# Twelve of sixteen experts in 64-slot pairs of plain float32 products, in turn with four split ones

## The chip, the cores and the metric

The program runs on one core of a Trainium2 chip. The metric is the device time of one execution in microseconds; the median of several executions is taken. Five engines run their own instruction streams beside each other: TensorE (PE, with its weight loads shown as PEld), VectorE (DVE), ScalarE (ACT), GpSimd (POOL) and SyncE (SP), which here issues the loads of the weights.

## What is computed

Two transformer blocks follow one another on 256 tokens of width 1024. The first has three token mixers and, behind them, a mixture of experts in two levels; the second has two layers with modulation from a conditioning vector. The change touches only the mixture of experts of the first block. Each token goes to one of four groups and, in it, to two of four experts:

```python
def hier_moe(h, wg, bg, we, be, w_gate, w_up, w_down):
    t = h.reshape(-1, D)                                  # 256 x 1024
    g_onehot = one_hot(argmax(t @ wg + bg), N_GROUPS)     # 4 groups, top 1
    ...                                                   # top 2 of the group's 4 experts
    y = jnp.zeros_like(t)
    for e in range(N_EXPERTS):                            # 16
        hid = jax.nn.silu(t @ w_gate[e]) * (t @ w_up[e])  # 1024 -> 256
        y = y + gates[:, e:e + 1] * (hid @ w_down[e])     # 256 -> 1024
    return y
```

All of it is float32. The inputs are drawn from a fixed seed; counted from them, the groups take 52, 33, 132 and 39 tokens, and their experts 25, 22, 40, 17; 18, 14, 19, 15; 32, 59, 82, 91; and 25, 11, 22, 20.

## The kernel before, in words

**Precision.** The kernel makes the product of two float32 matrices from three products in the type `float32r`: both operands are split into a high and a low part, and high x high, high x low and low x high are summed in PSUM. For a weight, ScalarE copies the high part (`hi`, L313) and VectorE subtracts it for the low part (`lo`, L317), in `split` (L300), from the raw tile that a DMA has brought (`raw`, 1 MB). Three pools hold the raw, high and low tiles; `rings` sets their number, (4, 4) in this stage: four raws and four each of hi and lo. `piece` takes a raw from a list of already loaded ones, or allocates one and issues its DMA on SyncE's queue, which waits there until the buffer is free.

**Routing.** `Moe.route` finds each token's group and experts, the group with most tokens and the order of the groups, which SyncE loads into registers, since the addresses of the weights hang on it. As soon as the first group is known, it issues four weight loads (L1659). Each token gets a slot, and `Pm` is the 0/1 matrix from tokens to slots. The largest group has four tiles of 128 slots, one for each expert. Each of the other three groups has one tile of 128 slots, which its four experts share: every one of them computes all slots, and its gate is zero where a token is not its own.

**Overflow.** If an expert of the largest group has, or another group has, over 128 tokens, `further` handles the rest under an `If` (L1813): a body of four experts written out one after the other.

**Gather, experts, scatter.** `gathered` multiplies the tokens (in high and low parts, `hh` and `hw`) by `Pm` and gives 8 chunks of 128 features for 512 slots (32 products of 512 columns), and later, at the fifth expert, for 384 slots (32 products of 384 columns). `slot_gates` multiplies `Pm` by the gates, 14 products (L1834). Then 16 experts run one after the other, and TensorE's order is laid by the scheduler along this list: `expert_in`, 8 chunks x 3 products of 512 columns (gate and up side by side, L1731 to L1733); `expert_out`, with the activation, two transposes (L1744), and 2 chunks x 2 halves x 3 products (L1754 to L1756), one expert behind. `rows_out` splits the result, and `scatter` (L1790) multiplies it by the transposed `Pm` and adds it to the residual `XT` (L1796): once for the four tiles of the largest group after its last expert, and once for the other three at the end. Behind it the first feed-forward part of the second block begins (`early`, product at L604), whose weights are issued at L297 as raws of a new pool.

The modulation products (`ada_mm`, L1060) are the one place of the kernel that already uses plain float32 products on a part of the columns of TensorE: 32 output rows each, up to four side by side.

Of the kernel before, what the change touches and what calls it, by code (L numbers as in the profile page):

```python
# [23 lines left out]
NC = 8  # L24
# [67 lines left out]
def _constants():  # L92
# [42 lines left out]
    k["iota"] = np.tile(np.arange(384, dtype=f) - 4095, (P, 1))  # L135
# [89 lines left out]
class Net:  # L225
# [406 lines left out]
    def first_block(self):  # L632
# [25 lines left out]
        self.ada_pool()  # L658
        es2, moe.T = self.phase("moe1")
# [899 lines left out]
class Moe:  # L1559
# [4 lines left out]

    def __init__(self, net, T):
        self.net, self.T, self.T0 = net, T, T
        nc = net.nc
        self.grep = T([P, 2 * D], "m8", 6)[:, :D]
        nc.sync.dma_start(self.grep, net.ap["grep"])
        self.hh, self.hw = T([P, 2, D], "m8", 6, F32R), T([P, 2, D], "m8", 6, F32R)  # L1570
        self.iota = T([P, 384], "iota")
        nc.sync.dma_start(self.iota, net.ap["k_iota"])
# [6 lines left out]
        self.pt = None  # L1579

# [22 lines left out]
    def route(self):  # L1603
# [4 lines left out]
        G = lambda a: a[:, :, :, None].to_broadcast([P, 2, 4, 5])  # L1608
# [13 lines left out]
        def first_max(src, m=None):  # L1622
# [9 lines left out]
            return m, oh  # L1632


        gm, goh = first_max(gl)
        cho = s(4, 5, dt=BF)
        V.tensor_copy(cho[:, :, :, 4], goh)
# [3 lines left out]
        for t in range(2):  # L1641
            nc.tensor.matmul(pk[:, 60:64], ones, cho[:, t, :, 4], start=(t == 0), stop=(t == 1))
# [11 lines left out]
        V.tensor_copy(order, qf)  # L1654
        load = lambda i: nc.values_load(order[0:1, i:i + 1], engines=(mybir.EngineType.SP,), min_val=0, max_val=3)
# [9 lines left out]
        em, o1 = first_max(se)  # L1665
# [7 lines left out]
        _, o2 = first_max(e2)  # L1673
        V.tensor_tensor(o1, o1, o2, OP.add)
        V.tensor_tensor(cho[:, :, :, 0:4], goh[:, :, :, None].to_broadcast([P, 2, 4, 4]),
                        o1[:, :, None, :].to_broadcast([P, 2, 4, 4]), OP.mult)
# [3 lines left out]
        nc.tensor.matmul(pk[:, 0:20], tri[:, 0:P], c0, start=True, stop=True)  # L1680
        nc.tensor.matmul(pk[:, 20:40], tri[:, P:256], c0, start=True, stop=False)
        nc.tensor.matmul(pk[:, 20:40], tri[:, 0:P], c1, start=False, stop=True)
        nc.tensor.matmul(pk[:, 40:60], ones, c0, start=True, stop=False)
        nc.tensor.matmul(pk[:, 40:60], ones, c1, start=False, stop=True)
# [9 lines left out]
        cnt = pk[:, 40:60].rearrange("p (g e) -> p g e", g=4)  # L1694
        V.tensor_reduce(sm, cnt[:, :, 0:4], AX.XY, OP.max)
        self.more = T([P, 1], "more", 1, I32)
        V.tensor_scalar(self.more, sm, 128.5, None, OP.is_gt)

        big, u, w = T([P, 4], "big"), T([P, 4], "cu"), T([P, 4], "cw_")
        V.tensor_scalar(big, gi[:, 0:4], b, None, OP.is_equal)  # L1700
        V.scalar_tensor_tensor(u, gi[:, 0:4], b, gi[:, 0:4], OP.is_gt, OP.subtract)
        V.tensor_scalar(w, big, -32.0, 32.0, OP.mult, OP.add)
        V.tensor_tensor(u, u, w, OP.add)
        pl5, place = s(4, 5), s(5)
        V.tensor_tensor(pl5, pk[:, 0:40].rearrange("p (t g e) -> p t g e", t=2, g=4), cho, OP.mult)
        V.tensor_reduce(place, pl5.rearrange("p t g e -> p t e g"), AX.X, OP.add)
        inb, ru, tmp = s(1), s(1), s(4)
        V.tensor_tensor(tmp, goh, big[:, None, :].to_broadcast([P, 2, 4]), OP.mult)
        V.tensor_reduce(inb, tmp, AX.X, OP.add)
        tmp2 = s(4)  # L1710
        V.tensor_tensor(tmp2, goh, u[:, None, :].to_broadcast([P, 2, 4]), OP.mult)
        V.tensor_reduce(ru, tmp2, AX.X, OP.add)
        self.slot = s(5)
        ob = s(4)
        V.tensor_tensor(ob, o1, B(inb), OP.mult)
        V.scalar_tensor_tensor(self.slot[:, :, 0:4], ob, -4096.0, place[:, :, 0:4], OP.mult, OP.subtract)
        V.scalar_tensor_tensor(self.slot[:, :, 4:5], ru, -128.0, place[:, :, 4:5], OP.mult, OP.subtract)

    def gate_up(self, w, e, j):
        return self.net.ap["egu"][bass.ds(w * 8 + (2 * e + j), 1)].rearrange("a p n -> (a p) n")  # L1720

    def expert_in(self, w, e, xh, xl, raw=None):
# [3 lines left out]
        for j in range(2):  # L1726
            for hi, lo, ks in net.piece(self.gate_up(w, e, j), 4, 512, raw):
# [8 lines left out]
    def expert_out(self, w, e, pg, gs, y, first, last, raw=None):  # L1736
# [3 lines left out]
        net.act(s, pg[:, 0:256], AF.Silu, scale=gs[:, 4:5])  # L1740
# [200 lines left out]
```

## Time and profile before

| what | value |
|---|---|
| median of 3 runs | 1452.15 us (1451.53 to 1452.27) |
| the profiled execution's own time | 1456.9 us |
| its span | 1455.1 us, mean granted clock 0.988 |
| TensorE, VectorE, ScalarE busy | 1411.1, 1138.2, 856.0 us |
| expert stage, first gate/up product to last scatter | 193.08 to 361.40 us |

The profile is of one execution, 4.75 us longer than the median. The span is the time between its first and last instruction. Busy time is the time in which an engine executes; instructions of TensorE overlap in its pipeline, so the time from one start to the next tells what one costs in a row, and the mean duration is longer.

### The profile page before, as it was taken

To read this page: it belongs to the slowest core of one execution; us is meant where nothing else is said; L and a number is where in the kernel's file an instruction comes from. 1 tells how busy PE (TensorE), PEld (TensorE's weight loads), DVE (VectorE), ACT (ScalarE), POOL (GpSimd) and SP (SyncE) were. 2 spreads that over 40 slices of the span, in tenths; PEclk is the share of its full clock that TensorE was granted. 3 is DMA by queue.
4 is the path that set the end of the run, shared out by engine and by line. 5 is a ranking of instruction groups with operands and counts; after the bars stand their busy time and mean duration, and the time that the engine had idled before them with its cause. 6 is when DMAs were issued, how large, how long until landed. Compare 5 with 4: busy or idle time off the path is not lost.

```text
span 1455.1 us, 22278 instructions
## 1 busy us (share of the span) xinstructions
PE 1411.1 (97%) x8093; PEld 1145.8 (79%) x8093; DVE 1138.2 (78%) x2557; ACT 856.0 (59%) x1575; POOL 0.2 (0%) x4
## 2 busy tenths in 40 slices
PE   7999699999999999999999999999999999999997
PEld 6755478778888888676788889888888677888886
DVE  8996478888999667485899886998687586887664
ACT  7545277777756555364755555666555464766553
POOL 0000000000000000000000000000000000000000
PEclk9999889999999999999999999999999999999999
DMA  8734557887887557543388686787477552275452
GB/s 306 276 129 165 236 202 261 298 324 275 326 318 271 198 184 266 194 169 116 136 294 309 226 297 214 284 315 261 159 263 290 211 194 87 90 241 191 158 179 69
DMA packets 51396, 326.67 MB, mean 224 GB/s; under 512 B 6209, under 2 KB 7378, under 8 KB 18898
## 3 DMA queue, kind: packets, MB, share of 16 engines
q1 hardware_dynamic: 50994, 325.00, 61.6%
q8 instruction: 65, 1.06, 0.3%
q14 instruction: 49, 0.40, 0.1%
q10 hardware_dynamic: 288, 0.20, 0.1%
HBM read 324.13 MB, written 1.05 MB: 223 GB/s over the span
## 4 chain that ended last, share of the span: by engine, by line
PE 79%; DVE 2%; ACT 2%; DMA 1%; issue 0%; DVEq 0%; ACTq 0%; SPq 0%
PE psd L337 12%; PE psa L337 11%; PE pse L337 10%; PE psd L339 7%; PE psa L339 6%; PE pse L339 5%; PE psd L353 2%; PE psm L1060 2%; PE psd L354 2%; PE psd L355 2%; PE psd L1732 1%; PE psd L1733 1%; PE psd L1731 1%; PE pse L1475 1%; PE pse L1754 1%; DVE lo L317 1%
## 5 line engine op out<-in xcount | busy, mean ns | idle before, releaser
L317 DVE TENSOR_TENSOR lo<-raw,hi 128x512 fp32r<-128x512 f32 x992 | 605.1, 639 | 164.9 <-ACT hi L313 162.6
L313 ACT ACTIVATE hi<-raw 128x1024 fp32r<-128x1024 f32 (+3 forms) x498 | 485.1, 980 | 347.7 <-PE psd L337 80.7
L337 PE MATMUL psd<-hl,hi 128*128 128x512 f32 x624 | 225.0, 402 | 7.8 <-ACT hi L313 7.0
L339 PE MATMUL psd<-hl,lo 128*128 128x256 f32 x656 | 185.0, 284 | 0.0
L337 PE MATMUL psa<-hl,hi 128*128 128x512 f32 x464 | 165.2, 397 | 1.2 <-ACT hi L313 1.2
L337 PE MATMUL pse<-hl,hi 128*128 128x512 f32 x464 | 164.3, 396 | 0.0
L337 PEld LDWEIGHTS psd<-hl,hi 128*128 128x128 f32 x624 | 117.9, 190 | 40.1 <-ACT hi L313 8.5
L339 PE MATMUL pse<-hl,lo 128*128 128x256 f32 x512 | 143.0, 280 | 0.0
L339 PE MATMUL psa<-hl,lo 128*128 128x256 f32 x496 | 138.7, 281 | 0.0
L339 PEld LDWEIGHTS psd<-hl,lo 128*128 128x128 f32 x656 | 124.7, 190 | 1.9 <-DVE lo L317 0.9
L337 PEld LDWEIGHTS psa<-hl,hi 128*128 128x128 f32 x464 | 87.2, 188 | 22.6 <-ACT hi L313 1.9
L337 PEld LDWEIGHTS pse<-hl,hi 128*128 128x128 f32 x464 | 87.3, 188 | 20.8 <-ACT w L384 0.3
L339 PEld LDWEIGHTS pse<-hl,lo 128*128 128x128 f32 x512 | 96.5, 189 | 0.2
L339 PEld LDWEIGHTS psa<-hl,lo 128*128 128x128 f32 x496 | 93.6, 189 | 0.8 <-DVE lo L317 0.4
L1089 DVE SCALAR_TENSOR_TENSOR acc<-araw,cact,acc 128x512 f32<-128x512 f32 x118 | 85.8, 748 | 1.6 <-DMA araw<-wada 1.6
L353 PE MATMUL psd<-hi,hl 128*128 128x512 f32 (+3 forms) x224 | 84.4, 377 | 0.8 <-ACT hl L375 0.4
L354 PE MATMUL psd<-lo,hl 128*128 128x512 f32 (+3 forms) x224 | 83.6, 373 | 0.0
L355 PE MATMUL psd<-hi,hl 128*128 128x512 f32 (+3 forms) x224 | 83.3, 374 | 0.0
L337 PE MATMUL psd<-hT,hi 128*128 128x512 f32 x220 | 77.6, 395 | 0.0
L337 PE MATMUL psa<-hT,hi 128*128 128x512 f32 x220 | 77.4, 394 | 0.0
L339 PE MATMUL psd<-hT,lo 128*128 128x256 f32 x264 | 74.2, 281 | 0.0
L339 PE MATMUL psa<-hT,lo 128*128 128x256 f32 x264 | 74.1, 281 | 0.0
(564 smaller groups left out, 2605.2 us busy)
## 6 DMA issues: line engine op xcount, KB each, us to landing
raw<-w SPq DMA_DIRECT2D x88, 1024.0 KB, 4.9
araw<-wada SPq DMA_DIRECT2D x64, 1024.0 KB, 6.7
raw<-w SPq DMA_DIRECT2D x64, 704.0 KB, 4.2
raw<-egu SPq DMA_DIRECT2D x32, 1024.0 KB, 5.0
raw<-edn SPq DMA_DIRECT2D x16, 1024.0 KB, 4.9
raw<-w2n SPq DMA_DIRECT2D x12, 1024.0 KB, 6.5
raw<-cw SPq DMA_DIRECT2D x8, 1024.0 KB, 5.8
araw<-wadb SPq DMA_DIRECT2D x8, 1024.0 KB, 5.7
```

Source lines behind the costliest of these rows:

```text
L313: nc.scalar.activation(hi[:, f:g], src[:, f:g], AF.Copy)
L317: ins = nc.vector.tensor_tensor(lo[:, f:g], src[:, f:g], hi[:, f:g].bitcast(F32), OP.subtract)
L337: nc.tensor.matmul(ps[:M, :].rearrange("p (a b) -> p a b", a=2), hi[:, o:o + M], xhl[:, k0 + k, :, :], start=st, stop=False)
L339: nc.tensor.matmul(ps[:M, 0:256], lo[:, o:o + M], xhl[:, k0 + k, 0, :], start=False, stop=sp)
L353: nc.tensor.matmul(o, xh, wh, start=st, stop=False)
L354: nc.tensor.matmul(o, xh, wl, start=False, stop=False)
L355: nc.tensor.matmul(o, xl, wh, start=False, stop=sp)
L1060: self.nc.tensor.matmul(self.ada_acc[32 * j:32 * j + 32, :], lhsT, rhs[:, 512 * j:512 * j + 512], start=start, stop=stop, tile_position=(0 ...
L1089: nc.vector.scalar_tensor_tensor(acc[:, w], raw[:, w], self.cact[:, c, 0:1], acc[:, w], OP.mult, OP.add)
L1475: nc.tensor.matmul(po[t][64 * g:64 * g + 64, 256 * rp:256 * rp + 256], vn[:, kt, v0:v0 + 64], pT[:, 256 * g:256 * g + 256], start=False, s ...
L1731: nc.tensor.matmul(pg, xh(c), wh, start=(c == 0), stop=False)
L1732: nc.tensor.matmul(pg, xh(c), wl, start=False, stop=False)
```

## The change

Slots: the largest group keeps four tiles of 128 slots, one for each expert, computed by split products as before (`split_in`, `split_out`). Every other expert gets 64 slots of its own, and two experts of a group share a tile of 128: six pair tiles. For a pair tile (`whole_in`, `whole_out`, through `whole`) the weights are used straight from `raw`, as plain float32, without a split: expert 1's product goes to columns 64 to 127 of TensorE and output rows 64 to 127, expert 0's to 0 to 63, and a dependency without a semaphore (`after`) ties the second to the first in TensorE's order. There are 8 + 4 such pairs of products for a tile. The gather for each of the three groups makes 8 x 4 products of 256 columns, and its result stays in float32.

The ten tiles are worked in the order 0, 4, 1, 5, 2, 6, 3, 7, 8, 9 (0 to 3 are large, 4 to 9 pairs), each with its gate/up part, its down part one place later, and its scatter, with additions to the residual, two places later. Slot gates are made for ten tiles. The pools become six raws and three each of hi and lo for this stage, and (4, 5) after it, as before. In `route` the four register loads stand ahead of the weight loads, of which there are six, for tiles 0 and 4. The overflow pass is a loop of sixteen turns over the experts in plain float32, with limits of 128 and 64 slots. The list of tiles, the order and the pair of products in the diff:

```diff
+        self.rings(6, 3)
         es2, moe.T = self.phase("moe1")
...
-        for i in range(4):
-            raw = net.t(net.raw_p, [P, 2048], F32, "raw")
-            nc.sync.dma_start(raw, self.gate_up(self.order[0], i // 2, i % 2))
-            net.loaded.append((raw, 1024))
         self.order += [load(i) for i in range(1, 4)]
+        for j in range(2):
+            net.loaded.append((self.raw(0, 0, j), 1024))
+        self.loaded = {k: self.raw(*k) for k in ((1, 0, 0), (1, 1, 0), (1, 0, 1), (1, 1, 1))}
...
-        V.tensor_scalar(self.more, sm, 128.5, None, OP.is_gt)
+        V.tensor_scalar(self.more, sm, 64.5, None, OP.is_gt)
...
+    TILES = [(0, (e,)) for e in range(4)] + [(r, (2 * q, 2 * q + 1)) for r in range(1, 4) for q in range(2)]
+    WORK = (0, 4, 1, 5, 2, 6, 3, 7, 8, 9)
...
+    def whole(self, out, lhsT, rhs, es, start, stop):
...
+        prev = None
+        for h in (1, 0):
+            p = slice(64 * h, 64 * h + 64)
+            ins = nc.tensor.matmul(out[p], lhsT[:, p], rhs(h), start=start, stop=stop, tile_position=(0, 64 * h))
+            if prev is not None:
+                self.net.after(ins, prev)
+            prev = ins
+
+    def whole_in(self, r, es, x, raws=None):
+        pg = self.net.ps("d")
+        for j in range(2):
+            raw = [self.raw(r, e, j) if raws is None else raws(h, r, e, j) for h, e in enumerate(es)]
+            for k in range(4):
+                c = 4 * j + k
+                self.whole(pg, x(c), lambda h: raw[h][:, 512 * k:512 * k + 512], es, c == 0, c == NC - 1)
+        return pg
...
-        with net.tc.If(more > 0):
-            self.further(order[0], hh, hw)
+        with net.tc.If(more > 0, preferred_fallthrough_block=True):
+            self.further()
+        net.tc.no_sync_barrier()
...
+        for t in range(2):
+            nc.vector.tensor_tensor(Pm[:, t, 512:].rearrange("p (c n) -> p c n", n=64),
...
+        gs = self.slot_gates(lambda t, g: Pm[:, t, g * P:(g + 1) * P].bitcast(F32), self.TILES)
...
-        work = [(0, e, e, e, True, True) for e in range(4)]
-        work += [(1 + g, e, 4 + g, g, e == 0, e == 3) for g in range(3) for e in range(4)]
...
+        for i in range(n + 2):
+            if i < n:
+                g = self.WORK[i]
+                r, es = self.TILES[g]
+                if r and r not in x:
+                    x[r] = gathered(r)
...
+            if i >= 2:
+                g = self.WORK[i - 2]
+                PT = self.tokens(lambda t: Pm[:, t, g * P:(g + 1) * P])
...
+                self.scatter(ys.pop(g), PT, "aa" if i < n + 1 else "ddaa", None if i < n + 1 else after)
+            if 1 <= i <= n:
+                g = self.WORK[i - 1]
+                r, es = self.TILES[g]
+                y = self.whole_out(r, es, pgs.pop(g), gs[:, g]) if r else self.split_out(g, pgs.pop(g), gs[:, g])
+                ys[g] = self.rows_out(y, yos[i % 2])
...
-        for e in range(4):
-            PT7 = T([P, 7, 256], "PT", 1, F32R)
...
+        with net.tc.For_i(0, 16) as i:
```

The body under the `If`, which a run that doesn't take it has to jump over, has 365 instructions of TensorE before and about 90 after.

**TensorE, the gate/up part.** Before, in the fourth expert of the largest group (psd is the PSUM tile, hi and lo the parts of the weight, hl and xl those of the gathered tokens):

```order
L1755 MATMUL pse_2721<-lo_2740,ehT_2729 128x512
L1756 MATMUL pse_2721<-hi_2739,ehT_2729 128x512
L1731 MATMUL psd_2761<-hi_2769,hl_2544 128x512
L1732 MATMUL psd_2761<-lo_2770,hl_2544 128x512
L1733 MATMUL psd_2761<-hi_2769,xl_2545 128x512
L1731 MATMUL psd_2761<-hi_2769,hl_2544 128x512
L1732 MATMUL psd_2761<-lo_2770,hl_2544 128x512
L1733 MATMUL psd_2761<-hi_2769,xl_2545 128x512
```

After, from the last gather product of the first pair tile to the next large one (L1919 is the gather, L1779 a transpose, L1809 a product of a pair, xp the gathered tokens in float32):

```order
L1919 MATMUL psd_2214<-Pm_1838,m_263_1327 128x256 x2
L1779 MATMUL psm_2241<-blob,w_471_2238 128x128
L1809 MATMUL psd_2220<-raw_1771,xp_2171 64x512
L1809 MATMUL psd_2220<-raw_1769,xp_2171 64x512
...
L1809 MATMUL psd_2220<-raw_1775,xp_2171 64x512
L1809 MATMUL psd_2220<-raw_1773,xp_2171 64x512
L1779 MATMUL psm_2241<-blob,w_471_2238 128x128
L1766 MATMUL psd_2277<-hi_2280,hl_2016 128x512
L1767 MATMUL psd_2277<-lo_2281,hl_2016 128x512
L1768 MATMUL psd_2277<-hi_2280,xl_2017 128x512
```

Eight pairs stand in a row, the two products of each pair next to one another, and they read the raw tiles; the split products follow behind. Over the stage there are 17 such runs.

**SyncE, the loads in `route`.** Before (order is the tile with the groups' numbers, egu the gate/up weights):

```order
L1655 TENSOR_LOAD order_1710
L1655 ISA x2
L1659 ISA
L1659 DMA raw_1722<-egu 128x2048
...
L1659 DMA raw_1728<-egu 128x2048
L1655 TENSOR_LOAD order_1710
L1655 ISA x2
```

After:

```order
L1657 TENSOR_LOAD order_1722
L1657 ISA x2
...
L1657 TENSOR_LOAD order_1722
L1657 ISA x2
L1732 ISA
L1732 DMA raw_1765<-egu 128x2048
...
L1732 DMA raw_1775<-egu 128x2048
```

All four register loads have moved ahead of the first weight, and six weights stand where there were four.

**SyncE, the end of the stage.** Before (edn is the down weight, w_00 the first feed-forward weights, k_cmask and the following ones small tables, wada the modulation weights):

```order
L297 DMA raw_4120<-edn 128x2048
L297 DMA raw_4301<-w_00 128x2048
L297 DMA raw_4406<-w_00 128x2048
L297 DMA raw_4463<-w_00 128x2048
L1552 DMA k_cmask<-k_cmask 128x32
L1552 DMA k_comb<-k_comb 128x32
L1552 DMA k_vbm<-k_vbm 128x8
L1547 DMA w_939_4272<-k_sel 128x512
L1076 DMA araw_4286<-wada 128x2048
```

After:

```order
L1732 DMA raw_3176<-edn 128x2048
L297 DMA raw_3305<-w_00 128x2048
L1553 DMA k_cmask<-k_cmask 128x32
L1553 DMA k_comb<-k_comb 128x32
L1553 DMA k_vbm<-k_vbm 128x8
L1077 DMA araw_3290<-wada 128x2048
L1548 DMA w_708_3276<-k_sel 128x512
L297 DMA raw_3410<-w_00 128x2048
```

One feed-forward weight instead of three stands ahead of the small tables, and the second comes behind them and a modulation load.

## Rows read from the trace of the kernel before

**Rows 1.** The page: one busy line, and the chain's shares by engine

```profile
PE 1411.1 (97%) x8093; PEld 1145.8 (79%) x8093; DVE 1138.2 (78%) x2557; ACT 856.0 (59%) x1575; POOL 0.2 (0%) x4
...
PE 79%; DVE 2%; ACT 2%; DMA 1%; issue 0%; DVEq 0%; ACTq 0%; SPq 0%
```

**Rows 2.** Stretches: length; PE, PEld, DVE, ACT, POOL busy; clock; DMA share; GB/s

```profile
193.08:201.20 8.12, 8.12 (x24) 6.46 (x25) 2.97 (x6) 3.06 (x3) 0.00 (x0) 0.63 0.00 0
...
201.20:230.30 29.10, 27.46 (x121) 21.76 (x120) 27.56 (x48) 23.93 (x33) 0.00 (x0) 1.00 0.83 316
...
235.90:355.65 119.75, 117.36 (x549) 94.40 (x548) 103.34 (x177) 87.22 (x109) 0.00 (x0) 1.00 0.75 282
355.65:361.40 5.75, 5.75 (x49) 5.64 (x47) 2.57 (x5) 2.71 (x5) 0.00 (x0) 1.00 1.01 423
193.08:361.40 168.32, 164.30 (x767) 132.77 (x767) 141.62 (x244) 122.22 (x158) 0.00 (x0) 0.98 0.74 278
```

**Rows 3.** Timeline, TensorE in the expert stage: start, length, line, count

```profile
189.63 3.59 PE L1834 MATMUL psn<-r,Pm 128*128 128x5 f32 x28
...
230.53 0.52 PE L1823 MATMUL psa<-Pm,m 128*128 128x384 f32 x2
230.88 0.51 PE L1823 MATMUL psd<-Pm,m 128*128 128x384 f32 x2
...
249.81 2.06 PE L1790 MATMUL psn<-PT,m 128*128 128x256 f32 x16
251.71 0.40 PE L1732 MATMUL psd<-lo,hl 128*128 128x512 f32 x1
...
259.44 0.39 PE L1732 MATMUL psd<-lo,hl 128*128 128x512 f32 x1
...
260.36 0.39 PE L1733 MATMUL psd<-hi,xl 128*128 128x512 f32 x1
```

**Rows 4.** Timeline, TensorE: plain float32 products of 32 rows, and their followers

```profile
159.87 3.63 PE L1060 MATMUL psm<-araw,cact 128*32 128x512 f32 x30
...
1258.53 1.05 PE L1060 MATMUL psm<-araw,cact 128*32 128x512 f32 x4
1259.52 0.70 PE L463 MATMUL psn<-sq,k_ones 128*128 128x256 f32 x2
1260.14 1.04 PE L1060 MATMUL psm<-araw,cact 128*32 128x512 f32 x2
1261.12 0.39 PE L604 MATMUL pse<-hT,hi 128*128 128x258 f32 x1
```

**Rows 5.** Groups by line, 193 to 362: count, busy us, mean ns, idle before

```profile
L317 DVE TENSOR_TENSOR lo<-raw,hi 128x512 fp32r<-128x512 f32 x184 | 116.9, 688 | 15.9 <-ACT hi L313 13.9
L313 ACT ACTIVATE hi<-raw 128x1024 fp32r<-128x1024 f32 x94 | 97.7, 1060 | 34.8 <-PE psd L1733 16.8 <-issue 6.8 <-PE pse L1756 3.5
...
L1796 DVE TENSOR_TENSOR XT<-psn,XT 128x512 f32<-128x512 f32 x4 | 2.8, 688 | 0.4 <-PE psn L1790 0.4
```

**Rows 6.** The branch's own records: shortest, median and longest in ns, start, count

```profile
L1813 ACTq COMPARE_BRANCH  x1: 45/45/45, 171.5 to 171.5; - x1
...
L1813 PEldq COMPARE_BRANCH  x1: 6747/6747/6747, 172.2 to 172.2; - x1
```

**Rows 7.** Timeline: the first weight loads, and the end of the stage

```profile
167.58 2.16 SPq L1659 DMA_DIRECT2D raw<-egu  x4
...
353.62 1.29 SPq L297 DMA_DIRECT2D raw<-w  x3
...
359.81 2.01 ACT L313 ACTIVATE hi<-raw 128x1024 fp32r<-128x1024 f32 x2 [3.02 <-DMA raw<-w]
...
361.53 0.33 SPq L1552 DMA_DIRECT2D k_cmask<-k_cmask  x1
```

More of the change, by code (lines that the diff above doesn't have):

```diff
@@ new lines, in slots, with slot_gates @@
+    def slots(self, t, r, e, n, slot, out):
+        self.net.nc.vector.tensor_scalar(out, self.iota[:, :n], slot[:, t, r, e:e + 1], None, OP.is_equal)
+    def slot_gates(self, lhsT, tiles):
+        net, nc = self.net, self.net.nc
+        n = len(tiles)
+        ps = net.ps("n")
+        for g in range(n):
+            for t in range(2):
+                nc.tensor.matmul(ps[:, 5 * g:5 * g + 5], lhsT(t, g), self.ep[:, t, :], start=(t == 0), stop=(t == 1))
+        gs = self.T([P, n, 2], f"gs{n}")
+        pv = ps[:, 0:5 * n].rearrange("p (n c) -> p n c", c=5)
+        nc.vector.tensor_copy(gs[:, :, 1], pv[:, :, 4])
+        for g, (r, es) in enumerate(tiles):
+            for h, e in enumerate(es):
+                p = slice(64 * h, 64 * h + P // len(es))
+                nc.vector.tensor_tensor(gs[p, g, 0:1], pv[p, g, e:e + 1], gs[p, g, 1:2], OP.mult)
+        return gs
@@ L1726, in expert_in @@
         for j in range(2):
-            for hi, lo, ks in net.piece(self.gate_up(w, e, j), 4, 512, raw):
+            for hi, lo, ks in net.piece(self.weights(0, e, j), 4, 512):
                 for i, k in enumerate(ks):
@@ new lines, in whole_in, with whole_out @@
+    def whole_in(self, r, es, x, raws=None):
[6 more added lines that the diff above has]
+        return pg
+    def whole_out(self, r, es, pg, gs, raws=None):
+        net, nc = self.net, self.net.nc
+        pt = self.hidden(pg, gs)
+        hT = self.T([P, 256], "ehf", 2)
+        nc.scalar.activation(hT, pt[:, 0:256], AF.Copy)
+        y = [net.ps("e"), net.ps("e")]
+        raw = [self.raw(r, e, 2) if raws is None else raws(h, r, e, 2) for h, e in enumerate(es)]
+        for k in range(2):
+            for b in range(2):
+                o = 1024 * k + 512 * b
+                self.whole(y[b], hT[:, k * P:(k + 1) * P], lambda h: raw[h][:, o:o + 512], es, k == 0, k == 1)
+        return y
@@ L1776, in rows_out, with tokens, scatter @@
         return yo
-    def scatter(self, ys, PT, rings, after=None):
+    def tokens(self, pm, ring="m"):
+        net, nc = self.net, self.net.nc
+        pt = net.ps(ring)
+        for t in range(2):
+            nc.tensor.transpose(pt[:, t * P:t * P + P], pm(t).bitcast(F32), net.k["ident"])
+        PT = self.T([P, 256], "PT", 2, F32R)
+        nc.scalar.activation(PT, pt[:, 0:256], AF.Copy)
+        return PT
+    def scatter(self, y, PT, rings, after=None):
         net, nc = self.net, self.net.nc
@@ new lines, in run @@
+        for c in range(NC):
+            for src, dst in zip((hh, hw), xs):
+                pg = net.ps("x")
+                for t in range(2):
+                    nc.tensor.matmul(pg, src[:, t, c * P:(c + 1) * P], Pm[:, t, 0:512], start=(t == 0), stop=(t == 1))
+                if c % 2 or dst is xs[0]:
+                    nc.scalar.activation(dst[:, c, :], pg, AF.Copy)
+                else:
+                    nc.vector.tensor_copy(dst[:, c, :], pg)
+        for t in range(2):
+            nc.vector.tensor_tensor(Pm[:, t, 512:].rearrange("p (c n) -> p c n", n=64),
+                                    self.iota[:, None, :64].to_broadcast([P, 12, 64]),
+                                    self.slot[:, t, 1:4].rearrange("p r e -> p (r e)")[:, :, None].to_broadcast([P, 12, 64]),
+                                    OP.is_equal)
@@ L1886, in after @@
                 net.early(net.gs[0][:, 0:8], net.mod[0][:, 0:8], m + e)
[L1888 to L1897 removed]
+        n = len(self.WORK)
@@ L1909, in further @@
+            PT = self.tokens(lambda t: Pm[:, t])
+            x2 = [net.w512() for _ in range(2)]
+            x = lambda c: x2[c // 4][:, c % 4 * P:c % 4 * P + P]
             for c in range(NC):
                 pg = net.ps("a")
-                for i, src in enumerate((hh, hw)):
+                for k, src in enumerate((self.hh, self.hw)):
                     for t in range(2):
-                        nc.tensor.matmul(pg[:, i * P:(i + 1) * P], src[:, t, c * P:(c + 1) * P], Pm[:, t, :],
-                                         start=(t == 0), stop=(t == 1))
```

272 lines of the change are left out of this document (124 added, 148 removed).

## The prediction, made before the changed kernel ran

> **What bounds the kernel now.** I read the page's busy shares first, then the engine line of the chain of waits, then a table by stretch of the expert stage, then that stage's timeline. The shares put TensorE at 97% of the span and VectorE at 78%, and the chain runs through TensorE for 79% of the span [rows 1]. A whole-span share says little about one stage, so the table by stretch decides [rows 2]: from the first gate/up product at 193.08 to the end of the last scatter at 361.40 are 168.32 us, of which TensorE is busy for 164.30, VectorE for 141.62 and ScalarE for 122.22, with the DMA engines at 0.74. Only the first expert is different: its 24 products take 8.12 us at a granted clock of 0.63, a mixture of the two levels 1.2 and 2.4 GHz; afterwards the clock is 1.00. So the stage is a row of products on TensorE with few gaps, and the time it can lose is the time of the products taken out. The reader should see in the rows that VectorE and ScalarE, at 84% and 73% of the stage, are close behind: a cut on TensorE alone would have been stopped by them.
>
> **The products.** Warm, a split product of 512 columns starts every 0.23 us (260.36 less 259.44, four steps), a scatter product of 256 columns every 0.119 us (251.71 less 249.81, sixteen) and a gather product of 384 columns every 0.175 us (0.35 for two) [rows 3]. Before: 16 experts x 36 = 576 split products, 132.5 us; the first expert's slow clock, 8.12 - 24 x 0.23 = 2.6; 32 gather products, 5.6; 7 tiles x 16 = 112 scatter products, 13.3; 46 transposes, costed like a scatter product, 5.5. Sum 159.5 of the 168.3, so 8.8 us (5.5%) are gaps and short waits.
>
> After: four experts keep the split, 144 x 0.23 = 33.1 us, and the slow start, 2.6. The other twelve become six tiles with 12 pairs each, 72 pairs of plain float32 products on 64 + 64 output rows. No such pair is in the trace, but the same form with 32 rows is, in the modulation product [rows 4]: sixteen products, four side by side and each in two records, stand in 3.63 us from 159.87 on; less 0.2 for going in and the last one's way out, that is 0.858 us for a group of four; a pair takes 0.99 (1258.53 to the next instruction at 1259.52), and one alone 0.98 (1260.14 to 1261.12). One, two or four thus cost the same; what exceeds 0.858 in the short ones, 0.12, is leaving the mode. I take 0.858 for a pair in a run: 61.8 us. The bounds are this value and twice it, the products one behind the other. The order table shows 17 runs of such products between ordinary ones; at 0.2 us each for going in and out (0.12 seen on the way out, the rest for the way in) 3.4. The gathers for these tiles are 3 x 32 products of 256 columns, 96 x 0.119 = 11.4; the scatters 10 x 16 x 0.119 = 19.0; 40 transposes 4.8. Sum 136.1. With gaps in the same ratio, x 168.3/159.5, 143.6: **24.7 us less** than 168.3. The bounds for the gaps are none (136.1) and twice as many (151).
>
> The Trainium skill's page "TensorE: Matmul & The Clock Gate", section "Part 3: Packing small matmuls — row/col tiling", speaks against the full overlap: it gives 2.38x for three column tiles, 79% of ideal. A pair would by that take 1/0.79 = 1.26 of a lone product, an estimate from that page, and the sum would be 16 us worse. In this trace four side by side and one alone differ by the mode's exit alone, so I stay with the row.
>
> **The splits.** The groups by line [rows 5] price a 128x512 lo at 688 ns on VectorE and a 128x1024 hi at 1060 ns on ScalarE. Thirty-six of the 48 weights (12 experts x 3) lose four of the one and two of the other: 36 x 4 x 0.688 = 99 us of VectorE and 36 x 2 x 1.06 = 76 us of ScalarE. What is added on VectorE is 40 instead of 8 additions to the residual, 32 x 0.688 = 22 us, the float32 copy of half the gathers, and three more tile evacuations; ScalarE gains less. VectorE then stands near 75 us and ScalarE near 65 in a stage of 144: these edits save no time of their own, but they take away the second bound, so I cost them at nothing. The cover is TensorE's 136 us.
>
> **The front.** The slot gates are 28 records for 14 products in 3.59 us [rows 3], 0.256 each; ten tiles instead of seven need six more, in series before the first gate/up product: **+1.5**. The two wide comparisons and some fifteen small gate operations on VectorE stand beside the 32 gather products of the first part, and the gates need them only at the end of these: nothing, or about 2 us if they are late. The branch on TensorE takes 6747 ns, while ScalarE's takes 45 [rows 6]; everything behind waits for TensorE's. Its skipped body shrinks from 365 TensorE instructions, four copies, to some 90, a loop over one. Between none and all of 6.7 us goes; weights are streaming then, and six loads are queued instead of four, which could delay what the branch fetches. I take **-2.5**, nearer to none.
>
> The page "Runtime: NRT & Kernel Launch" of the Trainium skill, section "Instruction fetch mechanics", says that a taken branch stalls for a fetch when its target lies outside the current two-page window. By that rule a jump over 90 instructions would more often land inside, and the whole 6.7 would go, 4 us better than my sum.
>
> SyncE reads all four group numbers before it issues the first weight. Four loads are issued in 2.16 us from 167.58 on [rows 7]; three more register reads put the first off by some 1.6 us (0.54 each, an estimate from the pace of those issues), and the first use at 193 is far behind: nothing, as long as the stage's front is TensorE's.
>
> **The stream.** Forty-eight weights of 1 MB are needed as before. With 24.7 us less time they must come faster: 42 of them, 44.0 MB, after the first six, in about 140 us, is 315 GB/s. The stage moved 316 GB/s in 201 to 230 and 423 at its end [rows 2], so it fits, but not with much room. A large tile takes 36 x 0.23 + 16 x 0.119 = 10.2 us for 3 MB, a pair tile 12 x 0.858 + 1.9 + its half of a gather 1.9 = 14.1 us for 6. In turn that is 2.7 us per MB; in the last two tiles, both pairs, 2.35 against 2.48 at 423 GB/s and 3.3 at 316. Six buffers, the lead, cover half of these 12 MB. I take **+2** for this end, with bounds of 0 and the rival's 15.
>
> **The tail.** After the stage the first feed-forward weight is split at 359.81 after 3.02 us of waiting for its DMA, while the mask load waits until 361.53 for the pools to close and the three weights have been issued at 353.62 [rows 7]. In the changed order only one weight stands ahead of the mask, the small loads and one modulation load in SyncE's queue, and the second weight behind them. The end of the scatter then sets the second weight's issue, so TensorE has one weight's products to hide its landing: **+2**, between 0 and 5 (a load's latency).
>
> Together -24.7 + 1.5 - 2.5 + 2 + 2 = -21.7. The profiled run of 1456.9 us (span 1455.1) becomes 1435.2. That run lies 4.75 above the median 1452.15, so the median should be 1430.4: **1430**.
>
> **The rivals.** (1) The weight stream becomes the bound. For it: six buffers, of which a pair holds four until its products have read them, where a split frees its buffer early. Against: the present stage's 278 GB/s is what TensorE asked for, and 423 were reached. If it kept to the 282 GB/s of 235.90 to 355.65 [rows 2], the 44.0 MB would run from 190 for 156 us to 346; four more pairs, an evacuation and a scatter, 7 us, end the stage at 353 instead of 338: +15, **1445**. (2) Each pair is drained before the next one starts, because the tie or a semaphore stands between them: then the 0.2 us of a run is paid by each of the 72 pairs, 14.4 for 3.4, 11 us more: **1441**. Against it: in [rows 4] four groups one behind the other pay that 0.2 once. (3) **Slower than before**: the pairs run one behind the other, because their 64 columns or the semaphores on two weights serialize them. Then 72 x 0.858 = 61.8 us more: **1492**. It turns the sign once a third of the overlap is lost (21.7 of 61.8). The groups of 32 rows [rows 4] speak against it, and the tie keeps the two products of a pair next to each other in TensorE's order. (4) The change doesn't do what it says: the loop is taken. The inputs route 52, 33, 132 and 39 tokens to the groups; the largest group's fullest expert has 91 of 128 slots, any other at most 40 of 64. It isn't taken; if it were, 16 passes of over 15 us each would give some **1700**.
>
> **How the numbers follow.** Forecast 0.74, rival 1 0.12, rival 2 0.06, rival 3 0.05, rival 4 under 0.01; the rest, 0.03, is a sum of mishaps near no change. The forecast's own range: without gaps (-7.5), the whole branch gone (-4.2), no price for stream and tail (-4), 1414; with double gaps (+7.5), no gain at the branch (+2.5) and 5 in the tail (+3), 1443. The range also takes in rivals 1 and 2, the first without the branch's gain (+2.5): 1414 to 1447. This kernel's measurement can tell some 0.2%, 3 us, from no change. Faster: the forecast and rivals 1 and 2, 0.92; same 0.03; slower 0.05.
>
> **What would show it.** Right: six runs of 8 tied pairs of about 6.9 us each, two products starting within some ns; TensorE busy for over 90% of a stage of 140 to 150 us, VectorE near half. Wrong: a second product of a pair starting 0.4 us or more behind the first (rival 3), or a gap of 0.2 us between pairs (rival 2); TensorE idle ahead of a pair for a raw weight, most of all in the last two tiles (rival 1); TensorE's branch still near 6.7 us, or longer (the front); the first feed-forward product waiting for its weight by over 5 us (the tail).

## The result and the profile after

The changed kernel takes 1441.65 us (median of 4 runs, 1440.19 to 1442.73) against 1452.21 (1451.53 to 1452.63): a ratio of 0.9917, with a 95% interval of 0.9905 to 0.9930. It is 10.6 us faster. The forecast was 1430, 22 us faster; the range of 1414 to 1447 holds the time, but only half of the gain came.

The traced execution of the changed kernel took 1442.18 us, 0.5 over its median, with a span of 1440.4. The one of before lay 4.75 over its own. A second trace of before (run b_again, below) has a span of 1452.2, and I use both where they differ.

The page after, with the busy line and the chain's line that answer to [rows 1]:

```profile
PE 1396.0 (97%) x8063; PEld 1099.1 (76%) x8067; DVE 1072.8 (74%) x2452; ACT 782.7 (54%) x1503; POOL 0.2 (0%) x4
...
PE 82%; DVE 2%; ACT 2%; DMA 1%; issue 1%; DVEq 0%; ACTq 0%
```

The expert stage by stretch, in the columns of [rows 2] (length; busy of PE, PEld, DVE, ACT, POOL; clock; DMA share; GB/s): all of it, the idle part near its end, and the tail up to the first feed-forward product:

```profile
188.44:340.12 151.68, 144.60 (x730) 83.78 (x729) 75.58 (x144) 49.77 (x86) 0.00 (x0) 0.98 0.73 287
322.30:334.00 11.70, 9.37 (x40) 4.00 (x36) 3.52 (x7) 3.82 (x7) 0.00 (x0) 0.85 0.27 114
340.12:346.09 5.97, 4.53 (x18) 2.71 (x17) 4.72 (x12) 5.97 (x14) 0.00 (x0) 1.00 0.85 313
```

VectorE's work in the stage fell from 141.62 to 75.58 us and ScalarE's from 122.22 to 49.77, as the splits went (the prediction had 75 and 65). The stage is shorter by far less than they are: it is TensorE's.

Four differences make up the span. Each is the time from one mark in the trace to the next (first gate/up product; end of the last scatter; first feed-forward product; end):

| part | before, first trace | before, second trace | after | forecast of the difference | measured, by first and second trace |
|---|---|---|---|---|---|
| up to the first gate/up product | 193.08 | 192.28 | 188.44 | -1.0 | -4.6, -3.8 |
| expert stage, with the stream's term | 168.4 | 165.6 | 151.7 | -22.7 | -16.7, -13.9 |
| last scatter to first feed-forward product | 1.7 | 2.4 | 6.0 | +2 | +4.3, +3.6 |
| the rest of the kernel | 1092.0 | 1092.0 | 1094.3 | 0 | +2.3, +2.3 |
| span | 1455.1 | 1452.2 | 1440.4 | -21.7 | -14.7, -11.8 |

**The branch.** Its records after, to be read against [rows 6]:

```profile
L1888 ACTq COMPARE_BRANCH  x1: 45/45/45, 171.4 to 171.4; - x1
L1888 PEldq COMPARE_BRANCH  x1: 352/352/352, 172.2 to 172.2; - x1
```

TensorE's branch went from 6747 ns to 352. The first gather product starts at 174.25 instead of 179.31, 5.1 us earlier.

**The pairs.** The timeline of TensorE (start, length, line), first pair tile:

```profile
199.93 7.09 PE L1809 MATMUL psd<-raw,xp 128*64 128x512 f32 x32
206.95 0.33 PE L1779 MATMUL psm<-blob,w 128*128 128x128 f32 x1
```

Thirty-two records are 16 products of two passes; eight pairs take 7.02 us from start to next start. In it are 8 x 0.858 = 6.86 and the ways in and out. The two products of a pair start 6 or 7 ns apart, and the next pair 0.86 us on: full overlap, as the forecast had it.

### The profile page after: what moved, and what is told of

Its sections match the earlier page's. It is cut to its first block, busy times and chain, and to the rows that moved or that the text cites. A ratio compares the mean times of both kernels' runs of the same rounds, so it can differ in the third digit from the quotient of the medians.

```text
span 1440.4 us, 21952 instructions
## 1 busy us (share of the span) xinstructions
PE 1396.0 (97%) x8063; PEld 1099.1 (76%) x8067; DVE 1072.8 (74%) x2452; ACT 782.7 (54%) x1503; POOL 0.2 (0%) x4
## 4 chain that ended last, share of the span: by engine, by line
PE 82%; DVE 2%; ACT 2%; DMA 1%; issue 1%; DVEq 0%; ACTq 0%
PE psd L337 12%; PE pse L337 11%; PE psa L337 10%; PE psd L339 7%; PE pse L339 6%; PE psa L339 6%; PE psd L1809 3%; PE psd L353 2%; PE psd L354 2%; PE psm L1061 2%; PE psd L355 2%; PE pse L1809 2%; PE psa L1868 1%; PE pse L1476 1%; PE psa L1471 1%; PE psd L335 1%
## 5 line engine op out<-in xcount | busy, mean ns | idle before, releaser
L317 DVE TENSOR_TENSOR lo<-raw,hi 128x512 fp32r<-128x512 f32 x848 | 513.6, 629 | 157.5 <-ACT hi L313 157.1
L313 ACT ACTIVATE hi<-raw 128x1024 fp32r<-128x1024 f32 (+4 forms) x426 | 409.2, 964 | 333.0 <-PE pse L337 80.9
L337 PE MATMUL psd<-hl,hi 128*128 128x512 f32 x592 | 213.7, 402 | 8.0 <-DVE hl L641 6.8
L339 PE MATMUL psd<-hl,lo 128*128 128x256 f32 x640 | 180.7, 285 | 1.3 <-DVE lo L317 1.3
L337 PE MATMUL pse<-hl,hi 128*128 128x512 f32 x496 | 177.1, 398 | 0.0
L339 PE MATMUL psa<-hl,lo 128*128 128x256 f32 x512 | 143.2, 281 | 0.0
L337 PEld LDWEIGHTS psd<-hl,hi 128*128 128x128 f32 x592 | 111.8, 190 | 37.0 <-ACT hi L313 8.6
L337 PEld LDWEIGHTS pse<-hl,hi 128*128 128x128 f32 x496 | 93.9, 190 | 24.0 <-issue 2.5
L337 PEld LDWEIGHTS psa<-hl,hi 128*128 128x128 f32 x464 | 87.1, 188 | 24.2 <-ACT hi L313 3.1
L337 PE MATMUL pse<-hT,hi 128*128 128x512 f32 x220 | 77.6, 395 | 0.0
L339 PE MATMUL pse<-hT,lo 128*128 128x256 f32 x264 | 74.2, 281 | 0.0
```

Of the source, the lines that this page charges most:

```text
L313: nc.scalar.activation(hi[:, f:g], src[:, f:g], AF.Copy)
L317: ins = nc.vector.tensor_tensor(lo[:, f:g], src[:, f:g], hi[:, f:g].bitcast(F32), OP.subtract)
L337: nc.tensor.matmul(ps[:M, :].rearrange("p (a b) -> p a b", a=2), hi[:, o:o + M], xhl[:, k0 + k, :, :], start=st, stop=False)
L339: nc.tensor.matmul(ps[:M, 0:256], lo[:, o:o + M], xhl[:, k0 + k, 0, :], start=False, stop=sp)
```

## The experiments

**A second trace of before.**

> The kernel before, unchanged, for a second trace of it. Theory: the 6.7 us of TensorE's branch are paid in every execution; this trace shows 6 to 7 us there again and a span of 1450 to 1455 us. Rival: they belong to the one execution that was traced first, 4.75 us above the median; then the branch takes under 3 us here and the time is near 1452.

It took 1453.97 us. The branch, and the first expert and the whole stage by stretch:

```profile
L1813 PEldq COMPARE_BRANCH  x1: 6627/6627/6627, 172.7 to 172.7; - x1
```

```profile
192.28:197.80 5.52, 5.52 (x26) 4.53 (x26) 2.97 (x6) 3.19 (x3) 0.00 (x0) 1.00 0.10 43
192.28:357.89 165.61, 161.58 (x768) 130.69 (x767) 141.68 (x244) 121.46 (x158) 0.00 (x0) 1.00 0.75 284
```

The branch is the same, so it isn't what set the first trace apart. That trace's slow start is missing here: the first expert's 24 products took 8.12 us at a granted clock of 0.63 [rows 2], and here the first 5.52 us, 24 x 0.23, hold that many at 1.00. The first trace is 2.9 us longer than this one; 2.8 of them are in the stage, and 2.6 of these are the stretch of low clock at its start.

**Before, without the overflow branch.**

```diff
-        more = nc.values_load(self.more[0:1, 0:1], min_val=0, max_val=1)
-        with net.tc.If(more > 0):
-            self.further(order[0], hh, hw)
```

> The kernel before without the overflow pass and its branch (left out; these inputs never take it). Theory (every execution pays for the branch): 1452.2 - 6.5 = about 1446. Rival (only the traced execution paid): 1451 to 1452.5. A smaller gain, 1 to 3 us, would say that what waits behind the branch (weights, the activation table) is late anyway.

1444.92 us, 0.9942 of before (0.9926 to 0.9959): 7.2 us. So the branch is paid in full and nothing behind it takes its place. In the trace the first gather starts at 173.72 and the first gate/up product at 185.89, 6.4 us before that of the second trace of before. Leaving the branch out alone gives more than half of what the whole change gave. The changed kernel keeps a short branch, and the forecast had 2.5 us for it.

**The halves of a pair apart.**

```diff
-            for k in range(4):
-                c = 4 * j + k
-                self.whole(pg, x(c), lambda h: raw[h][:, 512 * k:512 * k + 512], es, c == 0, c == NC - 1)
+            self.apart([(pg, x(4 * j + k), lambda h, k=k: raw[h][:, 512 * k:512 * k + 512], es, 4 * j + k == 0,
+                         4 * j + k == NC - 1) for k in range(4)])
...
+        prev = None
+        for h in (1, 0):
+            p = slice(64 * h, 64 * h + 64)
+            for out, lhsT, rhs, es, start, stop in work:
+                ins = nc.tensor.matmul(out[p], lhsT[:, p], rhs(h), start=start, stop=stop, tile_position=(0, 64 * h))
+                if prev is not None:
+                    self.net.after(ins, prev)
+                prev = ins
```

> The changed kernel with the two products of a pair no longer side by side: four products of one half of the columns, then four of the other. Theory (the overlap comes from standing next to each other): a gate/up part has 16 products of 0.858 us with 3 borders at which two overlap, 13 slots instead of 8; a down part 7 instead of 4; 6 x 8 x 0.858 = 41 us more, 1483. Rival (TensorE overlaps halves however they stand): within 3 us of 1441.7.

1464.77 us in one execution, 23 us more, between the two expectations. The first pair tile on TensorE's timeline:

```profile
199.12 8.97 PE L1844 MATMUL psd<-raw,xp 128*64 128x512 f32 x32
208.01 0.33 PE L1779 MATMUL psm<-blob,w 128*128 128x128 f32 x1
```

8.89 us instead of 7.02, where 13 slots would be 11.2. The records show why: the first product of the second half starts at 200.889, when the third of the first half's four products starts (200.883). So TensorE takes up a product of the other half while two of the first are not yet done: at each of the 3 borders two products overlap two, which makes 10 slots, 8.58 us. Products that stand apart are partly hidden; side by side they are hidden whole.

**Without the tie.**

```diff
-            if prev is not None:
-                self.net.after(ins, prev)
-            prev = ins
```

> The changed kernel without the tie between the two products of a pair. Theory (the tie keeps them side by side; without it the order puts products of one half in a row, as in the run with the halves apart, 23 us longer): 3 to 15 us more, 1445 to 1457. Rival (the order is the same without it, or TensorE finds the other half's product a few places on): 1440 to 1443.

1439.48 us, ratio to before 0.9906 (0.9889 to 0.9922), which is the changed kernel's. The stage in its trace is 151.6 us, like the 151.7 with the tie, and its pairs still start 6 or 7 ns apart: the order is the same without it. In this order the tie is worth nothing.

**Half of the pair experts' bytes.**

```diff
-        self.net.nc.sync.dma_start(raw, self.weights(r, e, j))
+        if r:
+            self.net.nc.sync.dma_start(raw[:, :1024], self.weights(r, e, j)[:, :1024])
+        else:
+            self.net.nc.sync.dma_start(raw, self.weights(r, e, j))
...
-                self.whole(pg, x(c), lambda h: raw[h][:, 512 * k:512 * k + 512], es, c == 0, c == NC - 1)
+                self.whole(pg, x(c), lambda h: raw[h][:, 512 * (k % 2):512 * (k % 2) + 512], es, c == 0, c == NC - 1)
...
-                o = 1024 * k + 512 * b
+                o = 512 * b
```

> The changed kernel with half of each pair expert's weight left out: 0.5 MB loaded instead of 1 MB, and the products of the second half read the first half again, so TensorE's work stays. Theory (TensorE and its short waits bound the stage): 1439 to 1442. Rival (the weight stream cost the 8 us that the stage is longer than the sum): 1432 to 1436.

1440.82 us, ratio 0.9922 (0.9902 to 0.9941): no gain that can be told. Its stage moved 182 GB/s instead of 287 and took 148.8 us in the one trace. The weight stream doesn't hold the stage up by more than some 3 us; a stretch of low clock that cost 1.7 us near the end of the changed kernel's stage (below) is missing in this trace, which leaves about 1 of them.

**The large tiles first.**

```diff
-    WORK = (0, 4, 1, 5, 2, 6, 3, 7, 8, 9)
+    WORK = (0, 1, 2, 3, 4, 5, 6, 7, 8, 9)
...
-        self.loaded = {k: self.raw(*k) for k in ((1, 0, 0), (1, 1, 0), (1, 0, 1), (1, 1, 1))}
+        self.loaded = {}
```

> The changed kernel with the four large tiles first and the six pair tiles behind them, and only the two weights of tile 0 loaded in the routing part. Theory (a pair tile takes 6 MB in 14.1 us, 2.35 us per MB, which the stream at its fastest, 2.48 us, doesn't give; 36 MB in a row must wait for weights): 5 to 12 us more, 1447 to 1454. Rival (the stream is no bound even so, as half the bytes gained nothing): 1440 to 1444.

1443.57 us, ratio 0.9942 (0.9925 to 0.9958): 2 us more than the changed kernel, and the intervals touch. The stage in its trace is 154.3 us. In turn is at best a little better; six pair tiles in a row don't starve, and no wait of TensorE in this stage ends with a weight's DMA.

**A large tile last.**

```diff
-    WORK = (0, 4, 1, 5, 2, 6, 3, 7, 8, 9)
+    WORK = (0, 4, 5, 1, 6, 7, 2, 8, 9, 3)
...
-            x = net.t(net.hl_p, [P, NC, 512], F32, "hl")[:, :, 0:256] if r == 3 else T([P, NC, 256], "xp")
+            x = T([P, NC, 256], "xp")
```

> The changed kernel in the order 0, 4, 5, 1, 6, 7, 2, 8, 9, 3: pairs in twos, a large tile last, and the gathered tokens of all three groups in one buffer. Theory (the end of the stage has nothing to fill the waits between the last pair tiles, and TensorE's clock falls there; split products would fill them): 3 to 5 us less, 1437 to 1439. Rival (two pair tiles in a row want 12 MB in 28 us, and the weights come late three times): 1443 to 1448.

1440.95 us, ratio 0.9922 (0.9905 to 0.9938): neither. The same waits stand at other places; TensorE waits 2.9 us for VectorE's gated product ahead of the hidden transposes instead of 1.1.

**The slots' transposes earlier, in their own PSUM tile.** This came from the gaps that the next section lists.

```diff
+            if 1 <= i <= n:
+                g = self.WORK[i - 1]
+                PTs[g] = self.tokens(lambda t: Pm[:, t, g * P:(g + 1) * P])
...
-                PT = self.tokens(lambda t: Pm[:, t, g * P:(g + 1) * P])
+                PT = PTs.pop(g)
...
-    def tokens(self, pm, ring="m"):
+    def tokens(self, pm, ring="n"):
```

> The changed kernel with the transposes of a tile's slots made one place earlier and in a PSUM tile of their own (ring n instead of m, which the hidden transposes use). Theory (the stage is longer than its sum by TensorE's waits for ScalarE's copies out of that one tile: 1.47, 0.82, 0.75, 0.75 and 0.75 us in the trace): 4 us less, about 1437.5. Rival (whatever is next in line is late too, as the sum of waits at the end of the stage): 1440.5 to 1442.

1433.76 us, ratio to before 0.9872 (0.9856 to 0.9889): 8 us less than the changed kernel by the medians, 6.5 by the two ratios to before, and more than the 4 expected. At the place of the longest gap, the changed kernel first, then this one (the number in brackets is TensorE's idle time and its releaser):

```profile
229.68 0.44 PE L1852 MATMUL psm<-blob,Pm 128*128 128x128 f32 x2
231.38 1.21 PE L1868 MATMUL psa<-PT,m 128*128 128x256 f32 x8 [1.26 <-ACT PT L1854]
```

```profile
229.24 0.38 PE L1852 MATMUL psn<-blob,Pm 128*128 128x128 f32 x2
229.82 0.71 PE L1868 MATMUL psa<-PT,m 128*128 128x256 f32 x4 [0.20 <-DVE XT L1873]
```

And the stage as a whole:

```profile
187.33:332.54 145.21, 141.01 (x730) 83.75 (x729) 75.34 (x144) 50.00 (x86) 0.00 (x0) 0.99 0.77 301
```

**The pools kept.**

```diff
         es.close()
-        self.rings(*RINGS)
```

> The changed kernel whose pools stay at six raws and three each of hi and lo behind the expert stage, instead of being opened anew as (4, 5). Three feed-forward weights then stand in SyncE's queue ahead of the small tables and use raws as these come free. Theory (the first feed-forward product starts 6 us after the last scatter instead of 2, because its weights are issued only when the whole old pool is free): 3 to 4 us less, 1438. Rival (three hi and lo instead of five cost the feed-forward parts more than that): 1442 or more.

1441.93 us, ratio 0.9917 (0.9898 to 0.9936), the changed kernel's. The first feed-forward weight goes out at 331.02, and the first product starts 1.3 us after the last scatter instead of 6.0; the rest of the kernel, with three hi and lo, is then 8 us longer (1102.3 against 1094.3). This trace is of the slowest of four executions, 4 us above the median, and has about twice as much of the lower clock there, so not all of the 8 us is owed to the three hi and lo. Both expectations are seen, and in the median they cancel.

**The pools opened later**, on top of the slots' transposes:

```diff
         es.close()
-        self.rings(*RINGS)
...
+            if l == f == 0 and j == 3:
+                self.ada_pool()
+                self.rings(*RINGS)
+                self.ada_pool(2)
```

> The run with the slots' transposes in their own PSUM tile, and in addition the pools opened anew only at the fourth column tile of the first feed-forward part instead of right behind the expert stage. Theory (the tail's 4.7 us, which the run with the kept pools gained at first, stay gained when only a few splits go by three hi and lo): 3 to 4 us less than 1433.8, about 1430. Rival (the opening of the pools costs one landing of a weight wherever it stands): 1433 to 1436.

1435.96 us, ratio 0.9879 (0.9863 to 0.9896), no better than without. The tail is 1.8 us, and TensorE waits 3.4 us in one piece for a hi there. The wait for a weight's landing stands there now.

**The last hidden transposes behind the down products of the tile before**, on top of the slots' transposes, alone and with the later pools:

```diff
-            nc.tensor.transpose(pt[:, k * P:(k + 1) * P], hd[:, k * P:(k + 1) * P], net.k["ident"])
+            ins = nc.tensor.transpose(pt[:, k * P:(k + 1) * P], hd[:, k * P:(k + 1) * P], net.k["ident"])
+            if last is not None:
+                net.after(ins, last)
```

> The run with the slots' transposes in their own PSUM tile, and in addition the transposes of the last tile's hidden rows put behind the down products of the tile before it in TensorE's order. Theory (TensorE stands 1.26 us for VectorE's product there, with 3.5 us of ready pairs behind the waiting transposes): 1 to 2 us less than 1433.8, about 1432. Rival (the wait moves to the end, behind the down products): 1433 to 1435.

> Both of the last two edits together. Theory: their sum, about 1428 to 1429. Rival (each only moves a wait): 1433 to 1436.

1432.90 us, ratio 0.9860 (0.9844 to 0.9876), and 1433.54, ratio 0.9869 (0.9853 to 0.9886). In the first the stage is 143.7 us against 145.2, so the wait is gone; in the time it can't be told from 1433.76. (`last` is given for the last tile alone, and is the last down product of the tile before.) The fastest kernels of the study are these two and the one with the slots' transposes alone. The times don't tell the three apart: all are some 19 us under before and 8 to 9 under the changed kernel.

## Why the forecast was half right

**The sum, term by term.** Against the first trace the front came out 3.6 us better than forecast, the stage 6.0 worse, the tail 2.3 and the rest 2.3 worse; the step from the span to the median took another 4.2. Together that is the 11.2 us between 1430.4 and 1441.65. So a part of the nearness is errors that cancel: without the better front the miss would be 15 us.

**The products were right, the gaps between them weren't.** Adding, by line, the time from each TensorE record's start to the next one's start splits the stage of 151.7 us:

| kind | forecast, no gaps | after | slots' transposes moved |
|---|---|---|---|
| split products | 35.7 | 36.4 | 35.7 |
| pairs, with the ways in and out | 65.2 | 67.2 | 65.2 |
| gathers | 11.4 | 13.6 | 13.0 |
| scatters | 19.0 | 24.0 | 24.2 |
| transposes | 4.8 | 10.6 | 7.0 |
| sum | 136.1 | 151.7 | 145.2 |

The pairs' price, the term with the widest bounds, is hit. The step that failed is "With gaps in the same ratio": a twentieth of the products' time, 7.5 us, was put where 15.6 were to come, just beyond the upper bound (151 for the stage). TensorE stands idle for 4.0 us of the stage before and for 7.1 after; slower first steps and a stretch of low clock, both below, add to it. The gaps before were those of a kernel with long runs of split products, into which waits fit. The changed kernel has ten scatters instead of two, each behind a fresh transpose, a copy by ScalarE and four additions by VectorE, and it lets the slots' and the hidden transposes share one PSUM tile (ring m, one buffer), where before they took ring a with two. That is the list of the gaps over 0.6 us in its trace (from one start to the next, less what the first product costs by itself): 1.47, 0.75, 0.75 and 0.75 where a scatter waits for the copied slots or a transpose for the copy out of the shared tile, 0.76 and 0.73 where a scatter waits for the addition, 1.26 and 0.69 for the hidden rows, and 0.82 for a lo (the expectation of the run with the slots' transposes counted this last one with the shared tile). Moving the slots' transposes took 6.5 us out of the stage in the traces, which shows this cause: 3.6 of them are in the transposes, and 2.0 in the pairs, where a stretch of low clock is gone. The run made them earlier and gave them their own tile at once; which of the two does it isn't shown. What stays in the scatters (24.0 against 19.0) was not tried. About 2 us of it is a step the sum didn't have: from the first scatter product behind another form to the next start are 0.22 or 0.23 us instead of 0.12, some seventeen times.

A second loss stands behind two of these gaps. The end of the last pair tiles on the timeline:

```profile
319.33 3.65 PE L1809 MATMUL psd<-raw,hl 128*64 128x512 f32 x16
324.08 0.44 PE L1779 MATMUL psm<-blob,w 128*128 128x128 f32 x2 [1.09 <-DVE w L1776]
325.05 0.44 PE L1852 MATMUL psm<-blob,Pm 128*128 128x128 f32 x2 [0.53 <-ACT ehf L1828]
325.41 5.35 PE L1809 MATMUL pse<-raw,ehf 128*64 128x512 f32 x16
...
334.05 3.65 PE L1809 MATMUL pse<-raw,ehf 128*64 128x512 f32 x16
```

The same sixteen records, four pairs, take 3.65 us, then 5.35, then 3.65. Ahead of the slow ones TensorE had stood idle twice; in this stretch the granted clock is 0.85 on average, and single passes take 0.84 us instead of 0.43, the lower of the two levels. With the slots' transposes moved, the first of the two waits is still there and the second isn't, and the four pairs keep the upper level:

```profile
319.15 0.44 PE L1779 MATMUL psm<-blob,w 128*128 128x128 f32 x2 [1.09 <-DVE w L1776]
319.52 3.65 PE L1809 MATMUL pse<-raw,ehf 128*64 128x512 f32 x16
```

**The base was inflated.** The sum was made against one execution, whose stage was 168.4 us; the second trace shows 165.6. The forecast kept the slow start of 2.6 us in both sums (the changed kernel's trace has 1.7 of it, 7.22 us at 0.76 for the same 24 products) and took the 4.75 us between execution and median as an offset that both kernels share. It wasn't: the changed kernel's execution lies 0.5 above its median. That is the 4 us between -14.7 in the spans and -10.6 in the medians.

**The front was better.** "I take -2.5, nearer to none" was wrong: TensorE's branch lost 6.4 us, nearly all, and the first gather starts 5.1 to 5.4 us earlier (VectorE's branch now ends last). The rule of the Trainium skill's page "Runtime: NRT & Kernel Launch", section "Instruction fetch mechanics", that a taken branch stalls for a fetch when its target lies outside the current window, gave the whole stall as gone, and the trace agrees with that outcome: 352 ns over 90 instructions, 6627 and 6747 over 365. The edit changed two things at this branch, the length of the body and the argument `preferred_fallthrough_block=True` of the `If`. No run has one without the other, so it isn't shown which of them shortened the branch, nor where a limit in length would lie. The DMA queues inside TensorE's long branch, 172.25 to 179.0 in the first trace of before (packets, MB, share of the DMA engines):

```profile
q1 hardware_dynamic: 373, 2.78, 99.4%
q8 instruction: 1, 0.02, 1.0%
q14 instruction: 3, 0.02, 0.9%
```

The second trace has the same one and three packets of instructions there. In the changed kernel, from the start of its short branch to the first gather, 172.16 to 174.25, queue q1, the kernel's own transfers, alone moves anything. So instructions were loaded during the long branch and none during the short one; the trace doesn't say for which engine.

The six further gate products cost 0.9 us instead of 1.5 (the gates take 4.38 us to the first gate/up product, before 3.45).

**The tail was worse**, +3.6 to +4.3 where +2 with a bound of 5 had been put. Its queue, to be read against [rows 7]:

```profile
337.74 0.34 SPq L297 DMA_DIRECT2D raw<-w  x1
340.15 0.34 SPq L1553 DMA_DIRECT2D k_cmask<-k_cmask  x1
...
342.44 1.16 SPq L297 DMA_DIRECT2D raw<-w  x2
345.00 1.04 ACT L313 ACTIVATE hi<-raw 128x1024 fp32r<-128x1024 f32 x1
346.09 0.54 PEld L604 LDWEIGHTS psd<-hl,hi 128*128 128x128 f32 x4 [1.01 <-ACT hi L313]
```

The prediction looked at the second weight behind the mask. It was the first that came late: before, it was issued 7.8 us ahead of the end of the scatter, now 2.4 us. A pair tile's raws are read by TensorE itself up to the last product, at 337.7, where a split had freed them early, and the new pool waits for all of them. The run with the kept pools shows the cause: with it the tail is 1.3 us.

**The rest** is 2.3 us longer, and no edit is there. In the traces it goes with the granted clock. Leaving out the last few us of the kernel, TensorE's clock is at the lower level in two stretches of this part of the changed kernel's trace, near 357 and 589 us, and in one of either trace of before. The eleven traces whose pools are opened anew right behind the stage order themselves by that: without such a stretch the rest takes 1090.2 to 1091.2 us, with one 1092.0 to 1092.6, with two 1094.2 to 1094.8. So each costs about 2 us, and the 2.3 are one more of them. Around the first, the changed kernel, and then the run with the slots' transposes moved at the same place (the clock is the third figure from the end):

```profile
350.00:365.00 15.00, 13.13 (x75) 11.33 (x74) 13.62 (x34) 10.68 (x19) 0.00 (x0) 0.89 0.99 392
```

```profile
342.00:357.00 15.00, 13.25 (x84) 11.46 (x84) 15.00 (x38) 12.07 (x21) 0.00 (x0) 1.00 1.01 403
```

Ahead of the fall TensorE had stood idle for 1.87 us, up to 355.86, for a hi; no trace of before has a wait of over 1 us near there. The other run stood 1.75 us there and kept the upper level, so whether the wait brings the fall isn't shown. The term was put at nothing. An execution's own clock can't be forecast from one trace of before, but such a stretch belongs in the range.

**The rivals.** The weight stream is no bound (half the bytes, no gain that can be told), so its +2 isn't seen. The pairs are neither drained one by one nor serial. That rival 2's price, 1441 us, is the measured time is luck: drained one by one, eight pairs would take 8.5 us (8 x 1.058), and they take 7.02. The Trainium skill's page "TensorE: Matmul & The Clock Gate", section "Part 3: Packing small matmuls — row/col tiling", whose 2.38x for three column tiles is 79% of ideal, would have given 77.9 us for 72 pairs without their ways in and out (an estimate from that page); with them the trace shows 65.2 to 67.2, so for two tiles of 64 columns the trace disagrees.

## What to carry to other kernels

When a change replaces long runs of one product by short runs of several kinds, don't scale the gaps of the old order: list for each new short run what it waits for (a copy out of PSUM, an addition, a shared tile), and price that. Look for an instruction that is paid once on the path, such as a branch, and test it alone: here the kernel without it is 7.2 us faster, where the whole change gave 10.6. And trace the kernel before twice, since a sum against one execution takes over what that execution had by itself.

## What the runs showed that was not expected

- TensorE starts a product on the other half of its columns while two products on the first half are not yet done: four and four in a row take 8.89 us, where pairs take 7.02 and one behind the other would take 13.7 (16 x 0.858).
- The stretch of low granted clock at the start of the stage moves between executions: the first expert's products ran at 0.63 in one trace of before and at 1.00 in the other, and 2.6 us hang on it. One more such stretch makes the difference of the rest of the kernel.
- Opening the pools anew cost a weight's landing at both places tried: 6.0 us of tail right behind the stage, or 1.8 us of tail and one wait of 3.4 us at the fourth column tile of the feed-forward part.
